# The last gate of a decoder layer as seven products of halves, with its weight sums made by DMA in DRAM

## The chip, the cores and the metric

The kernel runs on one core of one Trainium2 chip. The metric is the device time of one execution in microseconds (us). Lower is better. The engines are named as in the profile: PE (TensorE, with PEld for its weight loads), DVE (VectorE), ACT (ScalarE), POOL (GpSimd) and SP (SyncE, which here only issues DMAs). A DMA that SP issues goes into queue q1, one that POOL issues into queue q0; both are worked off by the same 16 DMA engines.

## The reference

One layer of a decoder: attention with forget gates, a normalisation, an MLP with a causal convolution over its gate, a second normalisation, and at the end a gated embedding that is added to the stream. 512 tokens, width 1024, MLP width 2816, all in float32.

```python
x = layer_norm(DEEPNORM_ALPHA * x + mix, ln_mix_g[i], ln_mix_b[i])
ffn = conv_ffn(x, ffn_w_up[i], ffn_conv_w[i], ffn_conv_b[i], ffn_w_down[i])
x = layer_norm(DEEPNORM_ALPHA * x + ffn, ln_ffn_g[i], ln_ffn_b[i])
gate = jax.nn.sigmoid(x @ ple_w_gate[i] + ple_b_gate[i])
x = x + gate * (p[i] @ ple_w_proj[i])
```

The change concerns `x @ ple_w_gate[i]`, a product of 512x1024 by 1024x1024, and the bias behind it.

## The kernel before, in words

**Products of float32.** Every operand is cut into a high part (rounded to fp32r by ACT) and a low part (the rest, subtracted by DVE). `three` (L147) issues three PE products for each block of 128 rows: high x high, high x low and low x high.

**Weights.** The class `Weights` holds a list of units of up to 128x1024 floats (512 KB). SP loads a unit into one of four `raw` buffers (L93), ACT cuts `whi` (L123) and DVE `wlo` (L129) into one of five pairs of buffers. A few units in the MLP have their low part made by an accumulating DMA that POOL issues (L126). SP's queue is in order, and so is each engine.

**The start.** SP loads the transposed input in eight blocks (`xraw<-xT`) between the first weights (`raw<-wv`, `raw<-wqk`), and ACT and DVE cut each block (L339, L340). PE computes the first values (`pv`), the first projections (`pp`), then the other values in two further rounds. In between, `keep_load` and `keep_sums` (L399 to L426) load pairs of blocks of the MLP's first weights (`ka`, `kb`), let DVE make sums of them (L421 to L424) and write these to DRAM (`kept`) for later. The sums stand in DVE's order between the cuts of weights and the release of the projections' PSUM banks (L460, L462). POOL makes two masks at the very start (L325, L326, L304) and then multiplies the attention's probabilities by their row sums' inverses (L499).

**The MLP** runs in four parts. For some blocks its products are already done as seven products of halves instead of eight (a scheme of the Strassen and Winograd kind: sums of quarters of both operands are multiplied, and the results combined). DVE and ACT follow an order written out in the code from its second block on (`manual_schedule`, L883); POOL and SP follow the scheduler.

**The end.** The last sums of the MLP (`r`), the second normalisation, the transposes of its result (`flip`, L644: PE transposes, ACT makes `x2h`, DVE `x2l`), seven of the eight halves of the embedding (`pl`, L988), and the gate (L998): for each of 2 column halves and 4 tiles of 128 tokens, 8 blocks of rows, three products each into one PSUM bank. DVE adds the bias (L1008), ACT takes the sigmoid (L1009), DVE multiplies by the embedding (L1014) and adds the stream (L1015), and SP stores. The last tile's second half runs in two quarters, with its embedding at the very end.

Of the kernel before, what the change touches and what calls it, by code (L numbers as in the profile page):

```python
# [9 lines left out]
F32 = mybir.dt.float32  # L10
F32R = mybir.dt.float32r
BF16 = mybir.dt.bfloat16
AF = mybir.ActivationFunctionType
# [3 lines left out]
P = 128  # L17
# [125 lines left out]
def trunk_layer(ctx: ExitStack, tc: tile.TileContext, xT, x2d, pT, wqk, wv0, wv1, wv2, bf, wo, wup, cwb,  # L143
# [108 lines left out]

    dram = ctx.enter_context(tc.tile_pool(name="dram", bufs=1, space=bass.MemoryType.DRAM))
    kept = {(j, q): dram.tile([P, 4, 512], F32, name=f"kept{j}_{q}") for j in KEPT for q in range(2)}
    u_up, u_dn = {}, [[] for _ in PAIRS]
    for part in range(4):
        fs = range(6 * part, min(6 * part + 6, NF))
# [32 lines left out]
    tl = slice(tiles[-1] * P, tiles[-1] * P + P)  # L290
    u_p1 = W.add(pT.rearrange("(k p) t -> p k t", p=P)[:, :, tl], n=2 * P, inner=P)
    u_pl1 = W.add(half_rows(wpl, 0, 2, 1), inner=512)


    zeros = base.tile([P, P], F32, name="zeros")
# [8 lines left out]
    nc.gpsimd.affine_select(ident, ones, pattern=[[1, P]], base=0, channel_multiplier=-1,  # L304
                            compare_op=ALU.is_equal, fill=0.0)

    neghalf = base.tile([P, 96], F32, name="neghalf")[:, :1]
    nc.vector.memset(neghalf, -0.5)


# [303 lines left out]
    def row(t, src):  # L614
        nc.sync.dma_start(t, src[0:1, :].to_broadcast([P, D]))
        return t
# [250 lines left out]

    before = None
    pending = []
    ordered = ExitStack()  # L870
    for part in range(4):
        ops = []
        slots = iter(CHUNKS[part] or ())

        def between():
            for _ in range(next(slots, 0)):
                next(before)

        for f in range(6 * part, min(6 * part + 6, NF)):
            q, j = f % 2, f // 2  # L880
            if f == 2:

                ordered.enter_context(tc.manual_schedule(  # L883
                    engines={mybir.EngineType.DVE, mybir.EngineType.Activation}))
            if q == 0 and j not in APART:
                E = hpool.tile([P, 8 * HALF], F32, tag="E", name=f"E{j}")
            if f == 0:
                a, b = slice(0, HALF), slice(HALF, S)
                up(0, 0, a)
                up(0, 1, a)  # L890
                up(1, 0, a, (3, x1h, x1l, xt))
                up(0, 0, b)
                up(0, 1, b)
                up(1, 0, b)
# [60 lines left out]
    x2l = post.tile([P, KD, S], F32R, tag="xl", name="x2l")  # L955
    for t in cut_tiles("X", 16, 1, "more", pool=hpool):
        extra.append(t.rearrange("p (a b) c -> p a (b c)", b=UNIT // HALF))
    for i, t in enumerate(tiles):
# [12 lines left out]
        if i == 0:  # L971
            W.cut_to(u_pl[1] + 1)
        if i > 1:
            flip(tiles[i - 2], x2h, x2l)


    pl = base.tile([P, NT, D], F32, tag="xl", name="pl")

    def embed(ps, up, ul, p0, pw, lo_c=0, w=512):

# [7 lines left out]
    for i, (n, t) in enumerate([(n, t) for n in range(2) for t in tiles][:-1]):  # L988
        ps = bank(f"pl{t}_{n}")
        embed(ps, u_p, u_pl[n], t * P, S)  # L990
        nc.scalar.activation(pl[:, t, n * 512:(n + 1) * 512], ps, AF.Copy)
        if i == 3:
            flip(0, x2h, x2l)


    bgs = row(cut_tiles("S", 4, 4, "bgs", F32)[0].rearrange("p a b -> p (a b)"), bg)

    def gate(n, t, lo_c=0, w=512):  # L998
        ps = bank(f"gt{n}{t}")[:, :w]
        c0 = slice(n * 512 + lo_c, n * 512 + lo_c + w)  # L1000
        tk = slice(t * P, (t + 1) * P)
        for k in range(KD):
            hi, lo = W.get(u_g[n][k // 2])
            c = slice(k % 2 * 512 + lo_c, k % 2 * 512 + lo_c + w)
            three(ps, hi[:, c], lo[:, c], x2h[:, k, tk], x2l[:, k, tk], k == 0, k == KD - 1,
                  weights_move=True)
        e = hpool.tile([P, S], F32, tag="a", name=f"ge{n}{t}_{lo_c}", bufs=2)[:, :w]
        nc.vector.tensor_add(e, ps, bgs[:, c0])  # L1008
        nc.scalar.activation(e, e, AF.Sigmoid)  # L1009
        return e  # L1010
# [7 lines left out]
    for n in range(2):  # L1018
        for t in tiles[:NT - n]:
            e = gate(n, t)  # L1020
            if n == 0 and t == tiles[0]:
                flip(1, x2h, x2l)
            finish(n, t, e, pl[:, t, n * 512:(n + 1) * 512])
    tz = tiles[-1]
    es = [gate(1, tz, c, 256) for c in (0, 256)]
    for e, c in zip(es, (0, 256)):
        ps = bank(f"pl{tz}_1{c}")[:, :256]
        embed(ps, u_p1, u_pl1, 0, P, c, 256)
        finish(1, tz, e, ps, c, 256)


def _layout(a):
# [45 lines left out]
```

## Time and profile before

| | |
|---|---|
| median of 3 runs | 651.94 us (651.73 to 652.17) |
| the profiled execution's own time | 651.7 us |
| its span | 650.0 us |
| PE busy | 644.2 us, 99% of the span |
| DVE busy | 520.8 us, 80% |
| ACT busy | 366.9 us, 56% |
| POOL busy | 93.6 us, 14% |
| moved by SP's queue | 105.77 MB |
| moved by POOL's queue | 3.15 MB |

Lines such as L152 are lines of the kernel. In a group, "out<-in xcount | busy, mean ns | idle before, releaser" gives the instructions of one line that write and read the named tiles, their busy time and their mean duration, then how long the engine sat idle before them and what ended that. In the chain of work that ended last, each row gives the start, the length and what ran. In the table of windows a row gives, for a stretch of time, the busy time and the number of instructions of PE, PEld, DVE, ACT and POOL, then the granted clock of PE, the mean busy share of the DMA engines and the GB/s moved. Starts of successive instructions of one engine can overlap with the end of the one before.

### The profile page before, as it was taken

How to read it: one execution, taken by the hardware profiler on the slowest of the kernel's cores; microseconds unless marked ns; L12 is line 12 of the kernel's file. 1: busy time of each engine (PE TensorE's matmuls, PEld its weight loads, DVE VectorE, ACT ScalarE, POOL GpSimd, SP SyncE). 2: the span in 40 equal slices, each digit the busy share in tenths (PEclk: the TensorE clock that was granted, in tenths of full speed). 3: DMA queues.
4: the chain of work that ended last, by engine and by line, in shares of the span. 5: the costliest groups of instructions: out<-in, count | busy, mean ns of one | idle time of the engine just before them, and what ended most of it. 6: DMA issues, size and time to landing. Idle time of an engine off the chain costs nothing.

```text
span 650.0 us, 10004 instructions
## 1 busy us (share of the span) xinstructions
PE 644.2 (99%) x3666; PEld 568.2 (87%) x3666; DVE 520.8 (80%) x854; ACT 366.9 (56%) x643; POOL 93.6 (14%) x85
## 2 busy tenths in 40 slices
PE   8999999999999999999999999999999999999997
PEld 7899888888888889889999988999988998888886
DVE  7764778988887599757899887789788998599464
ACT  6643777877785326946757554646545554425231
POOL 0000554454456021100000000000000000011000
PEclk9999999999999999999999999999999999999999
DMA  8764525445598315675665545663645562551321
GB/s 292 241 233 131 205 81 179 174 177 167 161 287 318 125 50 160 140 197 178 192 195 172 179 135 205 175 199 112 228 139 153 161 228 92 190 188 42 130 81 50
DMA packets 45858, 109.56 MB, mean 169 GB/s; under 512 B 4400, under 2 KB 8240, under 8 KB 45808
## 3 DMA queue, kind: packets, MB, share of 16 engines
q1 hardware_dynamic: 44944, 105.77, 49.7%
q0 software_dynamic: 864, 3.15, 2.6%
q8 instruction: 29, 0.48, 0.3%
q14 instruction: 21, 0.17, 0.1%
HBM read 96.19 MB, written 10.49 MB: 164 GB/s over the span
## 4 chain that ended last, share of the span: by engine, by line
PE 96%; DMA 2%; DVE 1%; SPq 1%; ACT 1%; issue 0%
PE g L152 18%; PE u L152 18%; PE pp L152 14%; PE x L152 8%; PE gt L152 7%; PE pv L152 7%; PE z L152 4%; PE r L152 3%; PE ap L152 3%; PE o L525 3%; PE t L512 2%; PE ao L152 2%; PE y L152 2%; PE s L475 2%; PE pl L152 2%; PE s L477 1%
## 5 line engine op out<-in xcount | busy, mean ns | idle before, releaser
L123 ACT ACTIVATE whi<-raw 128x1024 fp32r<-128x1024 f32 (+4 forms) x135 | 125.6, 938 | 87.0 <-PE pv L152 13.8
L129 DVE TENSOR_TENSOR wlo<-raw,whi 128x1024 fp32r<-128x1024 f32 (+4 forms) x130 | 137.5, 1067 | 31.4 <-ACT whi L123 30.4
L499 POOL TENSOR_SCALAR pr<-pr,rl 128x128 f32<-128x128 f32 (+1 forms) x64 | 75.5, 1195 | 132.1 <-DVE rl L495 132.1
L638 POOL TENSOR_TENSOR mv<-mv,neghalf 128x1 f32<-128x1 f32 x8 | 11.6, 1446 | 345.8 <-DVE mv L637 323.5
L152 PE MATMUL g<-x1h,whi 128*128 128x256 f32 (+1 forms) x168 | 54.7, 326 | 0.0
L152 PE MATMUL g<-x1l,whi 128*128 128x256 f32 (+1 forms) x168 | 54.4, 324 | 0.0
L152 PE MATMUL g<-x1h,wlo 128*128 128x256 f32 (+1 forms) x168 | 54.4, 324 | 0.0
L152 PE MATMUL u<-x1l,whi 128*128 128x256 f32 (+1 forms) x160 | 53.0, 331 | 0.0
L152 PE MATMUL u<-x1h,wlo 128*128 128x256 f32 (+1 forms) x160 | 53.0, 331 | 0.0
L152 PE MATMUL u<-x1h,whi 128*128 128x256 f32 (+1 forms) x160 | 53.0, 331 | 0.0
L152 PE MATMUL pp<-xh,wlo 128*128 128x512 f32 x128 | 50.5, 394 | 0.0
L152 PE MATMUL pp<-xh,whi 128*128 128x512 f32 x128 | 50.0, 391 | 0.0
L152 PE MATMUL pp<-xl,whi 128*128 128x512 f32 x128 | 50.0, 391 | 0.0
L491 ACT ACTIVATE pr<-s,nm 128x128 f32<-128x128 f32 (+1 forms) x64 | 33.5, 527 | 9.1 <-DVE nm L487 8.9
L152 PEld LDWEIGHTS g<-x1h,whi 128*128 128x128 f32 x168 | 32.0, 190 | 3.4 <-issue 0.7
L152 PEld LDWEIGHTS g<-x1l,whi 128*128 128x128 f32 x168 | 32.0, 190 | 2.6
L152 PEld LDWEIGHTS g<-x1h,wlo 128*128 128x128 f32 x168 | 32.0, 190 | 2.5
L152 PEld LDWEIGHTS u<-x1h,whi 128*128 128x128 f32 x160 | 30.4, 190 | 3.0
L152 PEld LDWEIGHTS u<-x1l,whi 128*128 128x128 f32 x160 | 30.4, 190 | 2.9
L152 PEld LDWEIGHTS u<-x1h,wlo 128*128 128x128 f32 x160 | 30.4, 190 | 2.8
L487 DVE CUSTOM_DVE_ANT_0 s<-s,mask 128x128 f32<-128x128 f32 (+1 forms) x64 | 30.0, 510 | 1.7 <-PE s L477 1.5
L123 ACT ACTIVATE whi<-side 128x512 fp32r<-128x512 f32 (+1 forms) x33 | 25.5, 782 | 9.7 <-PE u L152 3.6
(550 smaller groups left out, 1818.6 us busy)
## 6 DMA issues: line engine op xcount, KB each, us to landing
raw<-wup SPq DMA_DIRECT2D x34, 512.0 KB, 4.2
raw<-wdn SPq DMA_DIRECT2D x23, 512.0 KB, 3.8
raw<-wqk SPq DMA_DIRECT2D x16, 512.0 KB, 3.3
ka<-wup SPq DMA_DIRECT2D x8, 512.0 KB, 3.8
kb<-wup SPq DMA_DIRECT2D x8, 512.0 KB
kept<-kb SPq DMA_DIRECT2D x8, 512.0 KB, 3.5
kept<-ka SPq DMA_DIRECT2D x8, 512.0 KB, 3.1
raw<-wo SPq DMA_DIRECT2D x8, 512.0 KB, 4.3
```

Source lines behind the costliest of these rows:

```text
L123: self.nc.scalar.activation(hi[:, c:e], piece, AF.Copy)
L129: self.nc.vector.tensor_sub(lo[:, c:e], piece, hi[:, c:e].bitcast(F32))
L152: nc.tensor.matmul(ps, lhsT, rhs, start=start and n == 0, stop=stop and n == 2, skip_group_check=on)
L475: nc.tensor.matmul(ps[:, :n], QA[:, q], KA[:, :n], start=True, stop=False)
L477: nc.tensor.matmul(ps[:, :n], qb[0:68, q], kb[0:68, :n], start=False, stop=True)
L487: last_mask[:] = [nc.vector.tensor_tensor_reduce(ps[:, :w], ps[:, :w], mask[:, S - w:], -1.0, BIG, op0=ALU.add, op1=ALU.min, accum_out=nm[ ...
L491: nc.scalar.activation(pr[:, off:off + w], ps[:, :w], AF.Exp, bias=nm[:, i:i + 1], scale=-1.0, accum_out=ls[:, i:i + 1])
L499: nc.gpsimd.tensor_scalar_mul(pr[:, off:off + w], pr[:, off:off + w], rl[:, i:i + 1])
L512: nc.tensor.transpose(ps[:, w:w + P], pr[:, o:o + P], ident)
L525: nc.tensor.matmul(ps[:, q0:], V[:, j, h], p[:, o:o + w], start=j == 0 and n == 0, stop=j == NT - 1 and n == 1)
L638: nc.gpsimd.tensor_tensor(mv[:, 3:4], mv[:, 2:3], neghalf, op=ALU.pow)
```

## The change

The gate's product is split in halves three ways: rows of the weights (11, 12 above 21, 22), columns, and tokens (tiles 2 and 3 are the first half, 0 and 1 the second). Seven products of quarters replace eight, over 2 tiles each. In the code's names: x starts as the bias and takes a11 b11, then s2 t2, s3 t3 and a22 t4 on top; z starts as the sum of the two halves of the bias and takes s1 t1, then s4 b22; p2 is a12 b21. The bias is copied into PSUM by ACT before the first product, and products are added onto it. Copies of the sums in between are kept in SBUF (`g11`, `g12`, `g22`), and DVE combines them.

The sums of weights, t1 to t4, are made in DRAM tiles (`gt1` to `gt4`) by 16 DMAs that POOL issues: 8 plain copies and 8 accumulating ones, 512 KB each, in `gate_sums`. Ahead of each stands a copy of one column on ACT and one on POOL. The function is advanced twice for each of the MLP's blocks 6 to 13. The sums of the operand, s1 to s4, are made by DVE out of float32 copies of the transposed tiles, and cut by ACT and DVE (`second`).

```diff
+    gq = {f"t{n}": dram.tile([P, 4, 512], F32, name=f"gt{n}") for n in range(1, 5)}
+    steps = itertools.count(16)
+    def gate_sums():
...
+        for to, src in (("t1", "b11"), ("t2", "b22"), ("t1", "+b12"), ("t4", "b21"), ("t2", "+t1"),
+                        ("t3", "b22"), ("t4", "+t2"), ("t3", "+b12")):
+            for h in range(2):
+                m = next(steps)
+                nc.scalar.activation(small[:, m:m + 1], zeros[:, :1], AF.Copy)
+                nc.gpsimd.tensor_copy(small[:, m + 32:m + 33], small[:, m:m + 1])
+                if src[0] == "+":
+                    nc.gpsimd.dma_start(quad(to, h), quad(src[1:], h), accum_op=ALU.add)
+                else:
+                    nc.gpsimd.dma_start(quad(to, h), quad(src, h))
+                yield
...
-    u_g = [[W.add(half_rows(wg, 2 * j, 2, n), inner=512) for j in range(4)] for n in range(2)]
+    for g in ("b11", "b21", "t1", "t2", "b22", "t3", "t4"):
+        src = gq[g] if g in gq else half_rows(wg, 4 * int(g[1]) - 4, 4, int(g[2]) - 1)
+        u_g[g] = [W.add(src[:, 2 * j:2 * j + 2, :]) for j in range(2)]
...
+            if 6 <= f < 14:
+                next(beside)
+                next(beside)
...
+    def embedding(n, t, seed=None):
+        ps = bank(f"pl{t}_{n}", "six")
         embed(ps, u_p, u_pl[n], t * P, S)
         nc.scalar.activation(pl[:, t, n * 512:(n + 1) * 512], ps, AF.Copy)
+        if seed is not None:
+            nc.scalar.activation(ps, seed, AF.Copy)
+        return ps
...
+        s1, s2 = s12[:, :512], s12[:, 512:]
+        nc.vector.tensor_sub(s1, a21, pb)
+        nc.vector.tensor_sub(s2, s1, a11)
+        nc.scalar.activation(highs[0], s12, AF.Copy)
+        nc.vector.tensor_add(s4, a12, s2)
+        nc.vector.tensor_sub(s3, a11, a21)
+        nc.vector.tensor_sub(lows[0], s12, highs[0].bitcast(F32))
+        nc.vector.tensor_sub(x2l[:, 4:, tk], pb3, x2h[:, 4:, tk].bitcast(F32))
+        for v, c in ((s4, slice(0, 512)), (s3, slice(512, 1024))):
+            nc.scalar.activation(highs[1][:, c], v, AF.Copy)
+            nc.vector.tensor_sub(lows[1][:, c], v, highs[1][:, c].bitcast(F32))
...
     def finish(n, t, e, emb, lo_c=0, w=512):
         c0 = slice(n * 512 + lo_c, n * 512 + lo_c + w)
-        nc.vector.tensor_mul(e, e, emb)
-        nc.vector.tensor_add(y[:, t, c0], y[:, t, c0], e)
+        nc.scalar.activation(e[0], e[1], AF.Sigmoid)
+        nc.vector.tensor_mul(e[0], e[0], emb)
+        nc.vector.tensor_add(y[:, t, c0], y[:, t, c0], e[0])
...
+    x = [embedding(1, t, bgs[:, 0:512]) for t in firsts]
+    z = [embedding(1, t, b12) for t in seconds]
...
+    for i in range(2):
+        gate(x[i], i, "a11", "b11")
+        nc.scalar.activation(g11[i], x[i], AF.Copy)
+    second(1)
+    for i in range(2):
+        p2 = bank(f"p2{i}", "six")
+        gate(p2, i, "a12", "b21", on=False)
+        nc.vector.tensor_add(g11[i], p2, g11[i])
+        finish(0, firsts[i], (g11[i], g11[i]), emb(0, firsts[i]))
+    for i in range(2):
+        gate(z[i], i, "s1", "t1")
+        nc.scalar.activation(g22[i], z[i], AF.Copy)
...
```

POOL's order at the start of the program, before. The rows give the line, the operation, the tile written and the tile read, its size, and the semaphores waited for; `pr` are the probabilities of the first head, `rl` the inverses of their sums:

```order
L325 MEMSET mask 128x384
L326 ISA
L326 AFFINE_SELECT mask<-zeros 128x128 [waits DVE_49]
L304 AFFINE_SELECT ident<-ones 128x128 [waits DVE_49]
L499 TENSOR_SCALAR pr_704<-pr_704,rl_727 128x128 [waits DVE_49]
```

The same place on POOL now. `gt_71` is t1, `gt_72` t2, `gt_74` t4 and `gt_73` t3; a row with x2 stands for both halves; DMASW are the semaphores of POOL's own DMAs:

```order
L332 AFFINE_SELECT ident<-ones 128x128 [waits DVE_49]
L276 DMA gt_71<-wg 128x2x512 x2
L276 DMA gt_72<-wg 128x2x512 x2
L274 DMA gt_71<-wg 128x2x512 [waits DMASW0_49]
L274 DMA gt_71<-wg 128x2x512 [waits DMASW1_49]
L276 DMA gt_74<-wg 128x2x512 x2
L274 DMA gt_72<-gt_71 128x1024 [waits DMASW4_49,DMASW2_49]
L274 DMA gt_72<-gt_71 128x1024 [waits DMASW5_49,DMASW3_49]
L276 DMA gt_73<-wg 128x2x512 x2
L274 DMA gt_74<-gt_72 128x1024 [waits DMASW6_49,DMASW0_49]
L274 DMA gt_74<-gt_72 128x1024 [waits DMASW7_49,DMASW1_49]
```

All 16 DMAs (two more accumulates into `gt_73` follow) stand between the masks and the first multiplication; they wait for each other alone. POOL's 16 one-column copies stand elsewhere, behind the accumulating loads of the MLP:

```order
L126 DMA wlo_2974<-wup 128x1024 [waits DVE_49,Activation_49]
L126 DMA wlo_3017<-wup 128x1024 [waits DMASW0_49,PE_49,Activation_49]
L638 TENSOR_TENSOR mv<-mv,neghalf 128x1 [waits DVE_49,Pool_49] x4
L1074 UNCONDITIONAL_BRANCH
L1074 ISA [waits barrier_Pool_Activation_PE_DVE_SP_gather]
```

```order
L126 DMA wlo_2978<-wup 128x1024 [waits DVE_49,Activation_49]
L126 DMA wlo_3021<-wup 128x1024 [waits DMASW0_49,DMASW5_49,PE_49,Activation_49]
L272 COPY neghalf<-neghalf 128x1 [waits Activation_49] x16
L667 TENSOR_TENSOR mv<-mv,neghalf 128x1 [waits DVE_49,Pool_49] x4
L1191 UNCONDITIONAL_BRANCH
```

The first of these two is before, the second now: the copies came in there, and the DMAs did not move with them.

DVE's order where the gate begins, before: `wlo` are the low parts of the gate's weights, `ge` the gate of the first tile.

```order
L129 TENSOR_TENSOR wlo149_6149<-raw149_5925,whi149_6148 128x1024 [waits DMAHW6_49]
L129 TENSOR_TENSOR wlo150_6161<-raw150_5927,whi150_6160 128x1024 [waits DMAHW7_49]
L129 TENSOR_TENSOR wlo151_6173<-raw151_6119,whi151_6172 128x1024 [waits DMAHW0_49]
L129 TENSOR_TENSOR wlo152_6185<-raw152_6152,whi152_6184 128x1024 [waits DMAHW1_49,Activation_49]
L1008 TENSOR_TENSOR ge02_0_6196<-gt02_6147,bgsh_6144 128x512 [waits DMAHW2_49,PE_49]
```

The same place now: `bgsl` holds s1 and s2 of the third tile, `s430` its s4 and s3, `sg0` their low parts, `nt` the transposed tile in PSUM.

```order
L129 TENSOR_TENSOR wlo149_6139<-raw149_5982,whi149_6138 128x1024 [waits DMAHW6_49]
L1064 TENSOR_TENSOR bgsl_5934<-w21h_6136,nt_6169 128x512 [waits Activation_49]
L1068 TENSOR_TENSOR s430l_6183<-x2th_5931,w21h_6136 128x512
L1065 TENSOR_TENSOR bgsl_5934<-bgsl_5934,x2th_5931 128x512 [waits DVE_49]
L1070 TENSOR_TENSOR x2l_5928<-nt_6169,x2h_5927 128x4x128
L1067 TENSOR_TENSOR s430h_6182<-x2th_5931,bgsl_5934 128x512 [waits DVE_49]
L1073 TENSOR_TENSOR sg0l_6181<-s430l_6183,morel_5930 128x512 [waits Activation_49]
L1069 TENSOR_TENSOR sg0h_6180<-bgsl_5934,moreh_5929 128x1024 [waits Activation_49]
L1073 TENSOR_TENSOR sg0l_6181<-s430h_6182,morel_5930 128x512 [waits Activation_49]
L129 TENSOR_TENSOR wlo150_6238<-raw150_5984,whi150_6237 128x1024 [waits DMAHW7_49]
L129 TENSOR_TENSOR wlo151_6242<-raw151_6080,whi151_6241 128x1024 [waits DMAHW0_49]
L129 TENSOR_TENSOR wlo152_6256<-raw152_6143,whi152_6255 128x1024 [waits DMAHW1_49]
```

The eight operations on the operand's sums came in between the cuts of units 149 and 150. Up to the end of the MLP the orders of PE, DVE and SP are the same as before, and ACT's has the one-column copies added.

More of the change, by code (lines that the diff above doesn't have):

```diff
@@ L305, in trunk_layer @@
                             compare_op=ALU.is_equal, fill=0.0)
-    neghalf = base.tile([P, 96], F32, name="neghalf")[:, :1]
+    small = base.tile([P, 96], F32, name="neghalf")
+    neghalf = small[:, :1]
     nc.vector.memset(neghalf, -0.5)
@@ L869, in trunk_layer @@
     pending = []
+    beside = gate_sums()
     ordered = ExitStack()
@@ L957, in trunk_layer @@
         extra.append(t.rearrange("p (a b) c -> p a (b c)", b=UNIT // HALF))
+    firsts, seconds = tiles[:2], tiles[2:]
+    x2t = {t: v.rearrange("p a (b c) -> p (a b) c", c=P)
+           for t, v in zip(firsts, cut_tiles("S", 4, 4, "x2t", F32))}
+    bgs, s12 = [v.rearrange("p a b -> p (a b)") for v in cut_tiles("S", 4, 4, "bgs", F32)]
+    row(bgs, bg)
     for i, t in enumerate(tiles):
@@ L973, in trunk_layer @@
         if i > 1:
-            flip(tiles[i - 2], x2h, x2l)
+            flip(tiles[i - 2], x2h, x2l, x2t)
+        if i == 2:
+            W.cut_to(u_g["b11"][0] + 1)
     pl = base.tile([P, NT, D], F32, tag="xl", name="pl")
+    b12 = pl[:, tz, 0:512]
+    nc.vector.tensor_add(b12, bgs[:, 0:512], bgs[:, 512:1024])
     def embed(ps, up, ul, p0, pw, lo_c=0, w=512):
@@ new lines, in embedding, with second @@
+        return ps
+    whole = cut_tiles("A", 2, 3, "w21", F32)
+    sg = []
+    def second(i):
+        t = seconds[i]
+        tk = slice(t * P, (t + 1) * P)
+        pa, pb = [bank("nt", "two") for _ in range(2)]
+        for n, ps in enumerate((pa, pb)):
+            for k in range(4):
+                nc.tensor.transpose(ps[:, k * P:(k + 1) * P], y[:, t, (4 * n + k) * P:(4 * n + k + 1) * P], ident)
+        a21 = whole[i].rearrange("p a b -> p (a b)")
+        nc.scalar.activation(a21, pa, AF.Copy)
+        pb3 = pb.rearrange("p (k c) -> p k c", c=P)
+        nc.scalar.activation(x2h[:, 4:, tk], pb3, AF.Copy)
+        a11, a12 = [x2t[firsts[i]][:, 4 * n:4 * n + 4, :].rearrange("p k c -> p (k c)") for n in range(2)]
+        lows = [v.rearrange("p a b -> p (a b)") for v in cut_tiles("S", 4, 4, f"sg{i}")]
+        highs = [v[:, (3, 0)[i], :] for v in extra]
+        s4, s3 = [v.rearrange("p a b -> p (a b)") for v in cut_tiles("A", 2, 3, f"s43{i}", F32)]
+        s1, s2 = s12[:, :512], s12[:, 512:]
[9 more added lines that the diff above has]
+            nc.vector.tensor_sub(lows[1][:, c], v, highs[1][:, c].bitcast(F32))
+        sg.append({g: [v[m // 2][:, m % 2 * 512:m % 2 * 512 + 512].rearrange("p (k c) -> p k c", c=P)
+                       for v in (highs, lows)] for m, g in enumerate(("s1", "s2", "s4", "s3"))})
@@ new lines, in gate @@
+    def gate(ps, i, a, u, on=True, lo_c=0, w=512):
+        if a in ("a11", "a12", "a22"):
+            t = (firsts, seconds)[int(a[1]) - 1][i]
+            n = 4 * int(a[2]) - 4
+            xs = [v[:, n:n + 4, t * P:(t + 1) * P] for v in (x2h, x2l)]
+        else:
+            xs = sg[i][a]
+        for k in range(4):
+            hi, lo = W.get(u_g[u][k // 2], 3)
+            c = slice(k % 2 * 512 + lo_c, k % 2 * 512 + lo_c + w)
+            three(ps[:, lo_c:lo_c + w], hi[:, c], lo[:, c], xs[0][:, k, :], xs[1][:, k, :], k == 0 and not on,
+                  k == 3, weights_move=True, on=on)
@@ L1024, in trunk_layer, with emb, a_tile @@
[L1024 to L1027, printed above, removed]
+    def emb(n, t):
+        return pl[:, t, n * 512:(n + 1) * 512]
+    def a_tile(name):
+        return hpool.tile([P, S], F32, tag="a", name=name, bufs=2)
+    W.cut_to(u_g["b11"][1] + 1)
+    for t in firsts:
+        embedding(0, t)
+    embedding(0, seconds[0])
+    second(0)
+    x = [embedding(1, t, bgs[:, 0:512]) for t in firsts]
+    z = [embedding(1, t, b12) for t in seconds]
@@ new lines, in trunk_layer @@
+    g12, g22 = [[v.rearrange("p a b -> p (a b)") for v in cut_tiles("A", 2, 3, n, F32)] for n in ("g12", "g22")]
+    g11 = [a_tile(f"g11_{i}") for i in range(2)]
+    for i in range(2):
[7 more added lines that the diff above has]
+        finish(0, firsts[i], (g11[i], g11[i]), emb(0, firsts[i]))
@@ new lines, in trunk_layer @@
+    for i in range(2):
+        gate(z[i], i, "s1", "t1")
+        nc.scalar.activation(g22[i], z[i], AF.Copy)
+    for i in range(2):
+        gate(x[i], i, "s2", "t2")
+        nc.scalar.activation(g12[i], x[i], AF.Copy)
+    for i in range(2):
+        gate(z[i], i, "s4", "b22")
+        nc.vector.tensor_sub(g12[i], z[i], g12[i])
+        finish(1, firsts[i], (g12[i], g12[i]), emb(1, firsts[i]))
+    for i in range(2):
+        gate(x[i], i, "s3", "t3")
+        nc.vector.tensor_sub(g22[i], g22[i], x[i])
+        finish(1, seconds[i], (g22[i], g22[i]), emb(1, seconds[i]))
@@ L1028, in trunk_layer @@
+    gate(x[0], 0, "a22", "t4")
+    finish(0, seconds[0], (a_tile("g21_0"), x[0]), emb(0, seconds[0]))
+    for c in (0, 256):
+        gate(x[1], 1, "a22", "t4", True, c, 256)
+    e = a_tile("g21_1")
+    for c in (0, 256):
+        ps = bank(f"pl{tz}_0{c}", "two")[:, :256]
         embed(ps, u_p1, u_pl1, 0, P, c, 256)
-        finish(1, tz, e, ps, c, 256)
+        finish(0, tz, (e[:, c:c + 256], x[1][:, c:c + 256]), ps, c, 256)
 def _layout(a):
```

31 lines of the change are left out of this document (7 added, 24 removed).

## The prediction

> **What bounds the kernel now.** I read the page first, then the chain that ended last, and only then the stages that the change touches: the last 60 us and, because of where the new transfers stand, the first 60.
>
> ```profile
> span 650.0 us, 10004 instructions
> PE 644.2 (99%) x3666; PEld 568.2 (87%) x3666; DVE 520.8 (80%) x854; ACT 366.9 (56%) x643; POOL 93.6 (14%) x85
> PE 96%; DMA 2%; DVE 1%; SPq 1%; ACT 1%; issue 0%
> ```
>
> TensorE (PE) is busy for 99% of the span and is 96% of the chain that ended last, so a matrix product taken away is time, unless its place is taken by a wait. The chain over the last stretch (start, length, what):
>
> ```profile
> 599.80 5.44 PE gt L152 x24
> ...
> 606.12 38.41 PE gt L152 x192
> 644.53 1.05 PE pl L152 x7
> ```
>
> 24 products of 128x512 take 5.44 us, 0.2268 us each, without a gap. The gate has 216 of them because the code runs its last tile in halves: 168 whole products and 48 half ones, as much as 192 whole.
>
> The start is bound otherwise. The first chain pieces and the stages by window (PE, PEld, DVE, ACT, POOL busy, clock, DMA share, GB/s):
>
> ```profile
> 4.07 4.56 DMA raw<-wv
> 9.37 6.82 PE pv L152 x52
> ...
> 30.14 4.88 PE pv L152 x28
> ```
>
> ```profile
> 0.00:5.00 5.00, 3.89 (x17) 2.74 (x18) 3.55 (x14) 2.54 (x4) 1.15 (x7) 1.00 0.55 154
> 5.00:10.00 5.00, 4.24 (x28) 3.43 (x28) 3.35 (x6) 3.22 (x6) 0.00 (x0) 1.00 0.98 304
> 10.00:16.00 6.00, 6.00 (x50) 6.00 (x49) 4.51 (x7) 4.61 (x7) 0.00 (x0) 1.00 1.02 393
> ```
>
> From 5 to 16 us the 16 DMA engines are full, with the loads of xT, wv and wqk alone. The chain goes through a load until 8.6 us, and after that PE is only just behind them.
>
> **The products taken away.** Before: 4 token tiles x 2 column halves x 8 blocks of rows x 3 parts = 192 whole products. After: 7 products of halves x 2 tiles x 4 blocks x 3 = 168. The embedding keeps 14 half-tile groups and the transposes stay 32. So 24 x 0.2268 = **5.4 us** less on PE, all of it in a stretch where PE never stops.
>
> **What the end has to hide.** VectorE (DVE) and ScalarE (ACT) get more work there. The groups of the last 61 us and DVE's windows:
>
> ```profile
> L129 DVE TENSOR_TENSOR wlo<-raw,whi 128x1024 fp32r<-128x1024 f32 (+1 forms) x10 | 11.0, 1140 | 1.4 <-ACT whi L123 1.4
> L1008 DVE TENSOR_TENSOR ge<-gt,bgsh 128x512 f32<-128x512 f32 (+1 forms) x9 | 5.7, 630 | 14.0 <-PE gt L152 13.9
> L655 DVE TENSOR_TENSOR x2l<-nt,x2h 128x512 fp32r<-128x512 f32 x6 | 4.0, 677 | 0.4 <-ACT x2h L654 0.4
> ```
>
> ```profile
> 590.00:600.00 10.00, 10.00 (x50) 8.38 (x49) 10.00 (x15) 5.05 (x10) 1.45 (x1) 1.00 0.19 52
> 600.00:610.00 10.00, 10.00 (x50) 8.38 (x49) 5.72 (x8) 4.12 (x6) 0.00 (x0) 1.00 0.57 170
> 610.00:620.00 10.00, 10.00 (x45) 8.28 (x45) 4.48 (x8) 2.62 (x4) 0.00 (x0) 1.00 0.14 54
> 620.00:630.00 10.00, 10.00 (x46) 8.26 (x44) 6.96 (x9) 3.40 (x5) 0.00 (x0) 1.00 0.29 105
> 630.00:640.00 10.00, 10.00 (x51) 8.52 (x50) 3.48 (x6) 1.09 (x2) 0.00 (x0) 1.00 0.14 52
> ```
>
> DVE gains 6 weight cuts (14 units for 8) at 1.14, 8 operand sums, 4 cuts of 512 and one bias sum at about 0.63, and 2 cuts of 1024 at 1.14; it loses 2 x2l cuts and 2 of 8 bias additions. That is 6.8 + 8.2 + 2.3 - 2.6 = 14.7 us more on 30.6 busy of 50. 45.3 us in the 44.6 that remain is tight, though some of it (the first cut, the bias sum) can lie before 590. Followed row by row, the order puts the operand sums of the first tile before the cuts of units 150 to 152, whose products start only after two whole gates; by these durations each cut is ready 0.5 to 3 us ahead. I take 0.3 us of waits, bounds 0 to 2.5 (a quarter of the sums and cuts, 8 us, coming late). ACT has 16 us of work in these 50 and gets some 20 more (copies, seeds of the bias, cuts): covered. If the cover goes, each late cut costs PE its lateness. POOL does nothing there. The final multiply, add and store are the same; the sigmoid that now reads PSUM is done before the last embedding.
>
> The 16 one-column copies on ACT, in the MLP, and on POOL behind them cost nothing: ACT is 56% busy and nobody waits for them.
>
> **Where the 16 transfers really stand.** The copies were meant to pace them, but no data ties a transfer to its copy. In the built order the copies stand behind the MLP's accumulates, and all 16 transfers stand right behind the two masks, with no wait on any compute engine. In the profile of before POOL has this there:
>
> ```profile
> 1.51 0.28 POOL L304 TENSOR_SCALAR_AFFINE_SELECT ident<-ones 128x128 f32<-128x128 f32 x1
> 68.54 4.80 POOL L499 TENSOR_SCALAR pr<-pr,rl 128x128 f32<-128x128 f32 x4 [66.75 <-DVE rl L495]
> ```
>
> So the transfers start at about 1.8 us, into the full engines. The trace has no DRAM to DRAM transfer; the nearest are six accumulating loads in the MLP, and one stretch shows them against SP's queue (packets, MB, share of 16 engines):
>
> ```profile
> q0 software_dynamic: 432, 1.55, 70.7%
> q1 hardware_dynamic: 450, 1.17, 29.1%
> ...
> wlo<-wup POOLq DMA_DIRECT2D x1, 512.0 KB, 9.0
> ```
>
> That is 277 to 288 us, engines full. Packet for packet the two queues take turns (432 against 450), and the accumulating queue holds the engines for 71% of the time: 0.707 x 11 / 1.55 = 5.0 us of all 16 engines per MB, against 2.7 for plain loads beside it. The queue SP fills at the start does this from 5 to 16 us, and these are what it carries until the last xT (issues up to 11.5 us):
>
> ```profile
> q1 hardware_dynamic: 2294, 3.87, 99.9%
> ```
>
> ```profile
> xraw<-xT SPq DMA_DIRECT2D x7, 256.0 KB, 3.7
> raw<-wqk SPq DMA_DIRECT2D x2, 512.0 KB
> raw<-wv SPq DMA_DIRECT2D x3, 272.0 KB, 5.0
> raw<-wv SPq DMA_DIRECT2D x2, 136.0 KB
> xraw<-xT SPq DMA_DIRECT2D x1, 192.0 KB
> xraw<-xT SPq DMA_DIRECT2D x1, 64.0 KB
> ```
>
> 3.87 MB in 11 us is 2.8 us per MB. 4160 KB are 4.26 MB, of which 0.77 (154 GB/s for 5 us) have landed by 5 us, so 3.5 MB, about 2,070 packets, are still to come. If POOL's queue gets a packet for each of these, it moves its first four copies (1,088 packets, 2.1 MB), the two accumulates into t1 (544, 1.05 MB) and most of the next two copies: 2.1 x 2.8 + 1.05 x 5.0 + 0.85 x 2.8 = 13.5 us. That is the upper bound for the delay of the last xT. The lower is zero, if POOL's queue always had gaps where SP's is empty. Between them: over 250 to 285 us, with waits between its transfers, POOL's queue held
>
> ```profile
> q0 software_dynamic: 764, 2.80, 44.1%
> ```
>
> and at 44% the 10 us of loads would take 10 / 0.56, 8 us more. I take 10: four copies can be issued without waiting for anything, so there are fewer gaps than there.
>
> The Trainium skill (DMA: Bandwidth & Descriptors, Anatomy of one DMA, SWDGE path) prices a software DMA at 2.0 us plus its bytes at 436 GB/s, with nothing extra for accumulating: an estimate of 3.2 us for 512 KB, where the row has 9.0 to landing. By that page the interleaved megabytes would cost at most 9.2 us, and the forecast would be some 3 us lower; the rows are of this chip and kernel, and I go by them.
>
> What the delay does: the last xT is cut and used at once.
>
> ```profile
> 16.18 0.61 ACT L339 ACTIVATE xh<-xraw 128x512 fp32r<-128x512 f32 x1
> 17.45 0.69 DVE L340 TENSOR_TENSOR xl<-xraw,xh 128x512 fp32r<-128x512 f32 x1
> 17.72 0.67 PE L152 MATMUL pv<-whi,xh 128*128 128x272 f32 x4
> ```
>
> The cut is ready at 16.8, PE takes it at 17.72: about 1 us of slack. PE's order is fixed, and what stands behind the last xT takes until 30.14 whatever came before. So **9 us** of the 10 shift everything (0 to 12.5).
>
> After that, the value products and their loads run beside the rest of POOL's transfers, 33 us of engine time in all (4.2 MB x 2.8 + 4.2 MB x 5.0). The cover is long but has one weak place: DVE's in-order sums of ka and kb.
>
> ```profile
> 26.37 0.67 DVE L421 TENSOR_TENSOR ka<-kb,ka 128x512 f32<-128x512 f32 x1
> 37.36 0.69 DVE L460 SCALAR_TENSOR_TENSOR QB<-pp,QA 64x512 fp32r<-64x512 f32 x1
> ```
>
> ```profile
> 46.64 0.33 PE L152 MATMUL pv<-whi,xh 128*128 128x384 f32 x1
> ```
>
> Behind L421 stand the projection's release at 37.4 and the cuts for the second half of the values, which PE starts at 46.64: 8.6 us of cover, and 9 more by the shift. Between the last xT and kb stand four loads of wv and ka: with kb about 1,370 packets (256 for a wv load in rows of 1.5 KB, 128 for one of ka or kb in rows of 4). At a packet for a packet POOL's queue puts in the rest of its copies and the next five accumulates, 1.25 MB x 2.8 + 2.7 MB x 5.0 = 17 us at most, so kb is 10 to 27 us late. Up to 17.6 is covered, and the middle, 18.5, is not quite. I take **1.5 us** of waiting, bounds 0 to 9.
>
> POOL itself is blocked by four dependent steps of about 9 us, to some 40 us; its first multiply is needed at 68.5. Covered, unless DRAM accumulates take twice as long.
>
> **Sum**, against the profiled execution's own 651.7 us (span 650.0): 651.7 - 5.4 + 0.3 + 9 + 1.5 = **657.1 us**. The median of the three runs is 651.94, 0.2 above that run; a difference under about 0.2%, 1.3 us, is not told from none.
>
> **Rivals.**
> 1. *The start hides the transfers.* POOL's queue lets SP's packets through, or its descriptors come slowly, so that the last xT is at most 1 to 4 us late. For: how the queues take turns was seen in one stretch alone, with larger rows on SP's side and with SP's queue perhaps not always full. Against: engines at 0.98 to 1.02 from 5 to 16 us, and 432 against 450 packets. It gives 651.7 - 5.4 + 0.3 + 0 to 4 = 646.6 to 650.6, and turns from gain to loss at a delay of about 5 us. The case that the transfers run in the MLP after all, as the copies intend, gives the same 646.6; against it stands the built order. Chance 0.21.
> 2. *DVE blocked behind kb.* kb is over 24 us late, DVE stands at its sum, and PE runs dry before the second values: 9 + 8 instead of 9 + 1.5, 663.6 (662 to 666). For: in-order sums, loads behind POOL's larger packets. Against: POOL's accumulates wait for each other, which leaves SP's queue alone in between. Chance 0.12.
> 3. *A draw*: the delay just about eats the gain, 650.6 to 653.2. Chance 0.07.
>
> The forecast itself, 653.2 to 662, has 0.60. That gives slower 0.72, same 0.07, faster 0.21. The range runs from the hidden case's lower end, 646.3, to 665, which takes in the blocked DVE; the likeliest case alone is 653.2 to 662.
>
> **What would show it.** Right: q0 packets from about 5 us on and over by 60; PE with several us of idle time before 30 us, released by DMA through whi or xh; the second values begun at 55 to 58 us instead of 46.6; the gate stretch 5 us shorter with PE full. Rival 1: at 46 to 51 us. Rival 2: PE waiting for DVE between 45 and 60 us, DVE waiting for kb. Wrong in the end stage: PE waits over 1 us for wlo or for the operand sums after 590 us. Wrong altogether: transfers seen in the MLP, or a PE that finishes the gate no earlier than its start moved.

## The result and the profile after

The changed kernel takes 669.43 us (median of 4 runs, 668.5 to 671.79), the kernel before in the same comparison 652.06 (651.73 to 652.17). The ratio is 1.027 (95% interval 1.024 to 1.030): slower by 17.4 us. The forecast had the direction, but 669.4 lies above its range of 646.3 to 665.0.

The profiled execution (own time 670.07 us), its span, its engines and the shares of its chain:

```profile
span 668.3 us, 10057 instructions
PE 644.9 (96%) x3630; PEld 567.0 (85%) x3630; DVE 533.1 (80%) x870; ACT 384.1 (57%) x685; POOL 117.4 (18%) x117
PE 79%; DMA 13%; ACT 3%; DVE 3%; issue 1%; SPq 1%; ACTq 0%; DVEq 0%
```

PE was idle for 650.0 - 644.2 = 5.8 us before and is for 668.3 - 644.9 = 23.4 now: 17.6 more. It is busy for 0.7 us more, although 5.4 us of products are gone, so the products that are left took 6.1 us longer. 17.6 - 5.4 + 6.1 = 18.3, the difference of the spans.

Where the time came from is told by one landmark: the products of the MLP's last sums (`r`), which stand in the same place of PE's order in both. This is their row (durations, then first and last start), before and after:

```profile
L152 PE MATMUL r<-whi,s9h x16: 388/390/477, 565.3 to 586.3; 128*128 128x512 f32 x16
```

```profile
L152 PE MATMUL r<-whi,s9h x16: 388/389/476, 588.6 to 609.6; 128*128 128x512 f32 x16
```

The last of them starts 23.3 us later. From there to the end it is 63.7 us before and 58.7 now: the new gate gains 5.0 us. So everything is lost ahead of that point, and the windows of the first 100 us hold it:

```profile
5.00:10.00 5.00, 1.39 (x11) 1.17 (x10) 0.97 (x2) 0.91 (x2) 0.32 (x1) 0.84 0.97 290
10.00:16.00 6.00, 3.45 (x13) 3.13 (x14) 2.18 (x4) 2.07 (x4) 1.59 (x2) 0.50 1.04 382
16.00:22.00 6.00, 6.00 (x39) 6.00 (x39) 2.94 (x6) 3.45 (x5) 0.00 (x0) 0.78 1.08 325
...
70.00:80.00 10.00, 3.88 (x18) 2.93 (x17) 3.99 (x4) 3.55 (x4) 1.15 (x1) 0.83 0.97 237
80.00:100.00 20.00, 14.62 (x56) 11.96 (x57) 13.32 (x31) 11.92 (x27) 6.24 (x6) 0.74 0.57 211
```

There are two holes in PE's work, one from 5 to 16 us and one from 70 to 90; in and behind each the granted clock is down to 0.5 to 0.84. From 100 us on PE is full again. The chain of waits through both holes:

```profile
3.12 9.11 DMA xraw<-xT
...
13.64 9.30 DMA xraw<-xT
...
43.10 13.70 DMA kept<-kb
56.82 7.78 DMA raw<-wv
...
65.09 8.85 DMA raw<-wqk
...
76.36 6.07 DMA raw<-wqk
...
84.85 0.48 DVE V L411
85.33 0.04 issue
85.38 8.07 PE pp L152 x24
```

The first hole is the late input that was forecast: the cut of the last block of the input starts 9.1 us late (16.18 before).

```profile
25.25 0.62 ACT L368 ACTIVATE xh<-xraw 128x512 fp32r<-128x512 f32 x1
```

The scores of the first head, which stand right behind the last values, begin at 71.5 us where they began at 63.3:

```profile
L504 PE MATMUL s<-KA,QA x8: 278/311/767, 71.5 to 93.9; 128*128 128x256 f32 x4, 128*128 128x384 f32 x2, 128*128 128x512 f32 x2
```

That is 8.2 us. The second hole makes the other 15, and it was not forecast. This is the start of the same projection in the chain of before:

```profile
64.74 5.46 PE pp L152 x24
```

It now starts 20.6 us late, 12.4 more than the scores, and its 24 products, at the low clock behind the hole, take 2.6 us longer. Its weights (`raw<-wqk`) are loaded from 65.09 on. The last step of the chain is DVE: `V`, for which PE waits, stands in DVE's order behind the cuts of these late weights. SP's own waits up to 95 us (in total, how often, the longest) name what held the load of values before them:

```profile
SPq L93 <- DMA kept<-kb: 10.8, 1, 10.8
```

SP's queue from 26 us on, before and after (start, length, line, transfer), shows it in place:

```profile
29.00 0.34 SPq L404 DMA_DIRECT2D kept<-kb  x1
31.59 0.33 SPq L404 DMA_DIRECT2D kept<-ka  x1
31.98 0.43 SPq L93 DMA_DIRECT2D raw<-wv  x1
...
40.37 9.26 SPq L93 DMA_DIRECT2D raw<-wqk  x4
```

```profile
43.10 0.34 SPq L433 DMA_DIRECT2D kept<-kb  x1
45.70 0.33 SPq L433 DMA_DIRECT2D kept<-ka  x1
56.82 0.38 SPq L93 DMA_DIRECT2D raw<-wv  x1
...
65.09 3.08 SPq L93 DMA_DIRECT2D raw<-wqk  x3
```

`kb` lies in one of the four raw buffers. The next load of values goes into that buffer, so it waits until the store `kept<-kb` has read it. Before, the store is issued at 29.00 and the load follows at 31.98. Now the store takes 13.7 us among POOL's transfers, the load waits, and behind it in SP's order the loads of wqk wait too: they go from 40.37 to 65.09, 24.7 us, while PE was 8.2 us late. Some 14 of these 24.7 us are the late `kb` itself, whose store is issued at 43.10 instead of 29.00, and nearly 11 are SP's wait for the slow store. From 40 to 57 us POOL's queue holds the engines for 79.0% of the time and SP's for 24.7%. The queues up to 90 us (packets, MB, share of 16 engines):

```profile
q1 hardware_dynamic: 6952, 14.51, 46.3%
q0 software_dynamic: 2816, 8.39, 46.1%
```

The 16 transfers held all engines for 0.461 x 90 = 41.5 us, not the 33 of the prediction, and they were not over by 60 us. POOL issues the last one here:

```profile
72.28 1.15 POOL L274 DMA_DIRECT2D gt<-wg  x1 [9.94 <-issue]
```

### The profile page after: what moved, and what is told of

Read it like the earlier page. It is cut to its first block, busy times and chain, and to the rows that moved or that the text cites. A ratio compares the mean times of both kernels' runs of the same rounds, so it can differ in the third digit from the quotient of the medians.

```text
span 668.3 us, 10057 instructions
## 1 busy us (share of the span) xinstructions
PE 644.9 (96%) x3630; PEld 567.0 (85%) x3630; DVE 533.1 (80%) x870; ACT 384.1 (57%) x685; POOL 117.4 (18%) x117
## 4 chain that ended last, share of the span: by engine, by line
PE 79%; DMA 13%; ACT 3%; DVE 3%; issue 1%; SPq 1%; ACTq 0%; DVEq 0%
PE g L152 17%; PE u L152 17%; PE pp L152 12%; PE x L152 7%; PE z L152 4%; PE r L152 3%; PE ap L152 3%; DMA xraw<-xT 3%; PE o L554 3%; PE t L541 2%; PE ao L152 2%; DMA raw<-wqk 2%; DMA kept<-kb 2%; PE y L152 2%; DMA kb<-wup 2%; PE pl L152 2%
## 5 line engine op out<-in xcount | busy, mean ns | idle before, releaser
L123 ACT ACTIVATE whi<-raw 128x1024 fp32r<-128x1024 f32 (+4 forms) x141 | 132.2, 943 | 115.8 <-DMA raw<-wv 26.5
L129 DVE TENSOR_TENSOR wlo<-raw,whi 128x1024 fp32r<-128x1024 f32 (+4 forms) x136 | 144.5, 1073 | 52.8 <-ACT whi L123 52.4
L667 POOL TENSOR_TENSOR mv<-mv,neghalf 128x1 f32<-128x1 f32 x8 | 11.6, 1447 | 211.6 <-DVE mv L666 189.3
L152 PE MATMUL pv<-whi,xh 128*128 128x384 f32 (+1 forms) x96 | 31.5, 340 | 6.5 <-ACT whi L123 6.2
L152 PEld LDWEIGHTS pp<-xh,wlo 128*128 128x128 f32 x128 | 24.6, 192 | 12.7 <-DVE V L411 7.5
## 6 DMA issues: line engine op xcount, KB each, us to landing
kept<-ka SPq DMA_DIRECT2D x8, 512.0 KB, 14.2
```

What stands on the lines that cost most here:

```text
L123: self.nc.scalar.activation(hi[:, c:e], piece, AF.Copy)
L129: self.nc.vector.tensor_sub(lo[:, c:e], piece, hi[:, c:e].bitcast(F32))
L152: nc.tensor.matmul(ps, lhsT, rhs, start=start and n == 0, stop=stop and n == 2, skip_group_check=on)
L667: nc.gpsimd.tensor_tensor(mv[:, 3:4], mv[:, 2:3], neghalf, op=ALU.pow)
```

## The experiments

Two theories stood at first. By theory 1 the sum of the engines' time decides: 41.5 us of transfers do not fit into the idle time of the first stretch. By theory 2 the order decides: a few loads that come late or wait for a slow store. Each ratio is to the kernel before on the same chip (651.97 to 652.13 us).

**The transfers held back (held).** Each transfer is ordered on POOL behind its copy, and so runs where the copy runs.

```diff
-                nc.gpsimd.tensor_copy(small[:, m + 32:m + 33], small[:, m:m + 1])
-                if src[0] == "+":
+                step = nc.gpsimd.tensor_copy(small[:, m + 32:m + 33], small[:, m:m + 1])
+                with tc.issue_after(step.ins):
+                    if src[0] == "+":
```

> The 16 transfers truly wait for their one-column copies, so they run in the MLP. Theory 1, the sum of the transfer time: the 16 transfers hold all 16 DMA engines for 41.5 us (46.1% of the first 90 us of the changed kernel), and what does not fit into the idle time of the engines pushes the loads back; in 300 to 450 us the engines of before are at 0.51 to 0.62, so some 65 us of 150 are idle and 41.5 fit: 646 to 648 us, and the start is again that of before (second values at 46.6 us). Theory 2, the order of the loads (late first loads, then one load that waits for a slow store of the sums kept): it has nothing to act on here either, 646 to 648. Rival 3, transfers of this kind slow the loads wherever they stand: over 650, with PE waits in the MLP.

Measured: 650.78 us (649.9 to 651.93), ratio 0.998 (0.997 to 0.999). The first scores begin at 64.0 us (63.3 before), and the loss is gone: it came from where the transfers stood. But it misses the 646 to 648 and has what rival 3 named, over 650 and PE waits in the MLP. PE's waits in this kernel:

```profile
PE u L152 <- DVE E L822: 1.1, 1, 1.1
...
PE pl L152 <- DVE g22h L1137: 1.0, 1, 1.0
PE g L152 <- DVE a L751: 0.4, 1, 0.4
```

Two transfers per block crowd the MLP: from 360 to 440 us the DMA engines are at 0.88 where they were at 0.58 before, and PE waits for 1.5 us for DVE. In the end PE waits 1.0 us, because `s3 t3` has to be read by DVE before `a22 t4` is added onto it. (The trace names PSUM banks after their last tenant, `pl`.)

**No transfers (none).**

```diff
-                nc.gpsimd.tensor_copy(small[:, m + 32:m + 33], small[:, m:m + 1])
-                if src[0] == "+":
-                    nc.gpsimd.dma_start(quad(to, h), quad(src[1:], h), accum_op=ALU.add)
-                else:
-                    nc.gpsimd.dma_start(quad(to, h), quad(src, h))
+                pass
...
-    for g in ("b11", "b21", "t1", "t2", "b22", "t3", "t4"):
-        src = gq[g] if g in gq else half_rows(wg, 4 * int(g[1]) - 4, 4, int(g[2]) - 1)
-        u_g[g] = [W.add(src[:, 2 * j:2 * j + 2, :]) for j in range(2)]
+    for to in ("b11", "b21", "t1", "t2", "b22", "t3", "t4"):
+        g = {"t1": "b11", "t2": "b22", "t3": "b12", "t4": "b21"}.get(to, to)
+        src = half_rows(wg, 4 * int(g[1]) - 4, 4, int(g[2]) - 1)
+        u_g[to] = [W.add(src[:, 2 * j:2 * j + 2, :]) for j in range(2)]
```

> The 16 transfers are left out and the gate reads plain quarters of its weights in place of their sums; the rest is as in the changed kernel. All theories: the end alone, 651.9 - 5.4 + 0.3 = 646 to 648. The difference between held and this kernel is what the transfers cost in the MLP: under 0.7 by theories 1 and 2, over 3 by rival 3.

Measured: 648.90 us (648.23 to 650.54), ratio 0.995 (0.994 to 0.997). That is above the 646 to 648: the end alone gains 3.2 us, not 5.1; its profile has 1.6 us of PE waiting for that read of `s3 t3`, inside the 0 to 2.5 us that the prediction gave the end. Held is 1.9 above it, between the 0.7 of theories 1 and 2 and the 3 of rival 3, so twice a block the transfers do cost something in the MLP; the last runs below show that this comes from the crowding.

**The transfers after the first loads (late).** The transfers stand behind a POOL copy that reads the last cut of the input; the rest is as in the changed kernel.

```diff
     value_rows(0)
+    x_in.append(nc.gpsimd.tensor_copy(small[:, 90:91], xl[:, KD - 1, S - 1:].bitcast(F32)).ins)
...
+                with tc.issue_after(x_in[0]):
```

> The first transfer waits for the cut of the last block of the input, so that the first loads (to some 17 us) have the engines to themselves. Theory 1: before had 16.0 us of idle engine time from 16 to 60 us and 7.4 more to 70, against 41.5 us of transfers, so the loads are pushed back by 18 to 25 us all the same, only later: 664 to 671 us, and the first values end as in before. Theory 2: the 8.2 us lost by the first loads are saved and the 13.5 us behind the slow store stay: 659 to 663. My prediction's main term, the late first loads alone: 646 to 650.

Measured: 668.07 us (667.47 to 669.35), ratio 1.025 (1.023 to 1.026). The number is theory 1's, but the rows are not. The first hole is gone as all said (14.21 us of PE work by 16 us, 14.12 before). What stops PE later are two things in order, not one in bytes: its waits, and SP's for the store:

```profile
PE t L544 <- POOL pr L531: 8.8, 4, 6.6
PE pp L152 <- DVE V L413: 7.6, 1, 7.6
```

```profile
SPq L93 <- DMA kept<-kb: 10.1, 2, 6.7
```

Started some 17 us later, POOL's chain of dependent transfers lasts beyond 90 us, and the first multiplications of the probabilities stand behind it on POOL. This run doesn't tell the theories apart.

**kb in a buffer of its own (kbuf).** Three padded tiles are made smaller to find the space.

```diff
-                  base.tile([P, UNIT], F32, name=f"kb{j}_{q}", tag="raw", bufs=RAW_BUFS))
+                  ap.tile([P, UNIT], F32, name=f"kb{j}_{q}", tag="keepb", bufs=1))
```

> The changed kernel, with the second block of each kept sum in a buffer of its own instead of one of the four raw buffers, so that no load of values waits for its store (10.8 us of SP's time in the changed kernel). Theory 1: the engines are full all the same, so the time stays within 3 us of the changed kernel, 666 to 671. Theory 2: the wait goes and with it most of the second stall of 13.5 us: 656 to 661.

Measured: 663.05 us (659.58 to 666.39), ratio 1.017 (1.012 to 1.021), below the one theory and above the other; the profile is of the slowest of its four runs. The edit did not do what was meant: the wait is not gone but has moved to the next load of `kb`, which now waits for the same store and has the loads of wqk behind it.

```profile
SPq L439 <- DMA kept<-kb: 13.0, 1, 13.0
```

**The transfers alone (bstart).** Before, with the call of `gate_sums` put behind the masks, without its copies.

```diff
                             compare_op=ALU.is_ge, fill=NEG)
+    for _ in gate_sums():
+        pass
```

> The kernel before, gate and all, with nothing added but the 16 transfers behind the two masks; nothing reads what they write. If the loss of the changed kernel is all in the transfers' place (theory 1, and theory 2 too), this shows it whole: the changed kernel's start is 23.3 us late (last sums of the MLP begun at 609.6 us against 586.3), so 652.1 + 23 = 673 to 677. Rival: a part of the loss is in the new gate, or the new gate hides some of it: under 672.

Measured: 673.55 us (670.68 to 677.28), ratio 1.033 (1.030 to 1.037). 21.6 us of loss without the new gate, where the changed kernel loses 17.4 with it: the loss is the transfers' alone, and the gate takes back some 4.

**Half of the transfers (half).**

```diff
+                if h:
+                    yield
+                    continue
```

> The changed kernel with the eight transfers of the first halves alone (the other halves of the sums are left out, plain quarters are read there). Theory 1: 20.7 us of engine time go into the 25.7 us that the engines of before are idle up to 70 us, so the wait for the second projections' weights goes; what stays is the delay of the first loads, 6 to 8 us, which PE can't make up: 648.9 + 6 to 8 = 654 to 657. Rival, a loss in proportion to the transfers: half of 20, 659 to 661.

Measured: 659.97 us (658.18 to 661.4), ratio 1.013 (1.011 to 1.015). The second hole is gone, as theory 1 said; the number is the rival's, because the first one is larger than in the changed kernel. The chain goes from the values to the scores without a stop, 11.6 us late (63.44 before):

```profile
41.75 33.30 PE pv L152 x192
75.06 0.23 PE s L508 x2
```

So the rival's number is luck. SP's queue shows why the second hole is gone:

```profile
43.98 0.34 SPq L437 DMA_DIRECT2D kept<-kb  x1
...
46.96 0.43 SPq L93 DMA_DIRECT2D raw<-wv  x1
```

The store is issued as late as in the changed kernel (43.10), but POOL's queue moves nothing from 40 us on, and the load of values follows 3.0 us behind the store, as it did before, with no wait for it. So a late `kb` alone makes no hole; it takes the slow store.

**Plain copies (plain).** `accum_op=ALU.add` is taken out of the accumulating transfers.

> The changed kernel with the eight accumulating transfers made plain copies (so the sums of weights are left out), same order, bytes and waits. In the changed kernel POOL's queue moved 212 GB/s at a share of 0.81 with copies alone (5 to 10 us), 3.8 us of all engines per MB, and 172 at 1.01 with accumulates (55 to 60 us), 5.9 per MB. By these the 16 copies cost 8.39 x 3.8 = 32 us against 41.5, and theory 1 gives 9 us less than the changed kernel: 657 to 662. Rival, an accumulate costs no more than a copy from DRAM to DRAM: 668 to 671.

Measured: 664.82 us (663.02 to 667.49), ratio 1.020 (1.018 to 1.022). Between the two again, but the price is plain. The queues up to 90 us:

```profile
q1 hardware_dynamic: 7197, 15.45, 49.3%
q0 software_dynamic: 2304, 8.39, 27.6%
```

Sixteen copies hold the engines for 24.8 us, 2.96 us per MB. The eight accumulates of the changed kernel then cost 41.5 - 12.4 = 29.1 us for 4.19 MB, 6.9 us per MB. The second hole isn't there: POOL's queue is empty by 50 us, the store is issued at 51.52, and the load behind it follows at 54.51. But the first has grown: the chain has the scores at 81.57, 18.1 us late.

```profile
54.88 26.69 PE pv L152 x154
81.57 0.23 PE s L504 x2
```

The traces suggest why cheaper transfers delay the first loads more. A transfer that ends sooner lets POOL issue the next one sooner: all 16 are issued by 38.41 us here, 10 in the changed kernel. From 20 to 40 us POOL's queue holds the engines for 63.8% of the time here, 53.1% in half and 42.6% in the changed kernel, and the first delays have the same order (18.1, 11.6, 8.2 us). No run tried it by itself.

**The store out of the way (kfree, bkfree).** kbuf, and besides the second round of loads of the sums kept and the first round of stores move from the second values to the first head's scores and after. The same two edits on the kernel before are the measure.

```diff
-    keep_sums()
-    keep_load()
     value_rows(2)
...
-            if s == 0 and h != 2:
+            if s == 0 and h != 2 or h == 3:
                 keep_sums()
                 keep_load()
```

> The changed kernel with the kept sums taken out of the way: kb in a buffer of its own, and the second round of loads and the first round of stores moved from the second values to the scores of the first head and after, so no load of values or of projections stands behind a store or waits for its buffer. In the changed kernel the scores begin 8.2 us late and the next projection 15 us later still. Theory 1 (what the engines carry decides): 2.1 MB at some 2.7 us per MB, 5.7 us, are gone from the stretch, so 9 of the 15 us stay: 662 to 666. Theory 2 (the order decides: the slow store and what waits for it): the 15 us go but for 2, 655 to 659.

> The kernel before with the same two edits on the kept sums, as the measure for the run above: no store delays it and PE has no wait there to lose, so 651 to 653 by both theories. If this moves by more than 1 us, the run above is read against it.

Measured: kfree 654.66 us (653.11 to 657.63), ratio 1.004 (1.003 to 1.006); bkfree 651.99 (651.31 to 652.26), ratio 0.999 (0.998 to 1.000). The edits change nothing by themselves, and take 14.8 of the 17.4 us out of the changed kernel. The DMA engines are as full as in the changed kernel (in steps of 10 us 0.89 to 1.08 from 30 to 70, 0.96 to 1.04 there), POOL's queue carries the same 8.39 MB at 44.9%, yet the second hole is nearly gone; PE's chain passes from the values to the next projection in under 3 us:

```profile
40.47 33.15 PE pv L152 x191
73.62 1.06 ACT whi L123
74.71 1.23 DVE wlo L129
75.93 0.48 DVE V L411
76.45 5.74 PE pp L152 x24
```

```profile
L152 PE MATMUL r<-whi,s9h x16: 388/389/476, 576.6 to 597.6; 128*128 128x512 f32 x16
```

The landmark is 11.3 us late instead of 23.3. With the quick stores of half and plain, that settles the second hole for theory 2: it is the loads behind the slow store of kept sums. Theory 1's 662 to 666, which allowed for the 2.1 MB moved out of this stretch, is out.

**One transfer to a block (spread, spreadonly).** The version that the runs pointed to: held, with the transfers one to each of blocks 6 to 21.

```diff
-            if 6 <= f < 14:
-                next(beside)
-                next(beside)
+            if f >= 6:
+                next(beside)
```

spread besides puts the products `s3 t3` ahead of `s4 b22`.

> A version meant to keep the gain: the transfers held behind their copies, one for each of the MLP's blocks 6 to 21 instead of two for each of 6 to 13, and in the gate s3 t3 goes before s4 b22, so that DVE has 5.4 us instead of 2.7 to read x before a22 t4 is added onto it. Held twice a block they cost 1.5 us of PE waits in the MLP, and the wait for that read was 0.3 to 1.6 us: with both gone, 648.9 - 1.4 = 647 to 649. If the transfers cost as much spread out: 649 to 650.5.

> The transfers held one to a block as in the run called spread, with the gate's order as in the changed kernel. If the 3.6 us between held and spread come from the spreading of the transfers, the MLP has no PE wait here and the end has its 0.3 to 1.6: 648 to 649. If they come from the gate's order: 649.5 to 651.

Measured: spread 647.18 us (647.02 to 648.74), ratio 0.993 (0.992 to 0.995); spreadonly 647.45 (646.46 to 648.9), ratio 0.992 (0.991 to 0.994). Both beat both kernels, before by 4.7 to 4.8 us; spread is inside its 647 to 649, spreadonly is even below its 648 to 649. Spreading does it: neither trace has a PE wait from 200 us to the end, with 16 more transfers in it, and the MLP's windows of spread are full:

```profile
250.00:400.00 150.00, 150.00 (x963) 136.90 (x963) 125.20 (x180) 93.83 (x148) 15.21 (x19) 1.00 0.67 194
400.00:550.00 150.00, 150.00 (x898) 134.09 (x897) 130.63 (x185) 81.79 (x135) 12.87 (x19) 1.00 0.71 201
```

The gate's order changes nothing that these runs can tell.

## Why the prediction was wrong

- **The products taken away and the end: right.** Forecast -5.4 + 0.3; the changed kernel's end is 5.0 us shorter, and the waits of the end were 0.3 us there (up to 1.6 in other runs, within the bounds of 0 to 2.5).
- **Where the transfers stand: right.** They start at the program's start, and with them held in the MLP the loss is gone (held, spread, spreadonly); bstart shows it without the gate.
- **The first loads: right.** Forecast 9 us out of 10 for the last block of the input, bounds 0 to 12.5; measured 8.2 out of 9.1 in the changed kernel, 11.6 in half. The bound does not hold for every such kernel: with plain copies it was 18.1.
- **After that: the step that failed.** The prediction said that the cover is long but has one weak place, DVE's sums of ka and kb, and took 1.5 us for it, bounds 0 to 9. The values did lose nothing there: kb's first sum was 14.1 us late, which is inside the forecast 10 to 27 and under the 17.6 of cover, and the values ran without a stop. The real place was one step on, in SP's queue: the store of the same sums holds a raw buffer, and the loads of values and projections stand behind it. It cost 15 us, 12.4 of standing and 2.6 of slower products behind. The prediction listed the loads between the last xT and kb, and asked who waits for the sums on DVE; it did not follow the buffer of `kb` to its next user, nor the store that has to read it. That order was in the trace of before, where the store is issued at 29.00 and the load at 31.98; that the store would take 13.7 us instead of at most 3 was not.
- **The price of an accumulate: too low.** 5.0 us per MB from one stretch; the changed kernel shows 6.9. Copies were right (2.8 for 2.96). With it the end of the transfers was too early: the prediction had POOL blocked to some 40 us and its queue done by 60, and the last issue is at 72.28. That this let the late store fall among the transfers fits half and plain, where POOL's queue was done before it; the price was not changed alone.
- **Rival 2 was near, and wrong.** It put kb's lateness on DVE, with 663.6 us. kb's sum was late (its first step at 40.47 where it was 26.37), but PE did not wait for it. Where PE did wait for DVE, later, DVE stood before the cuts of the late wqk.
- **The clock was left out.** The prediction added idle time alone. The products behind the holes ran at a granted clock of 0.5 to 0.84 and took 6.1 us longer. Only 2.6 of these can be put to the kernel's time: at 23.6 us, when the clock was back at 1.00, PE had stood another 0.3 us for a block of the input, so at the first hole the loads decided and not the clock.

## What to carry to other kernels

Background transfers are placed by the built order, not by the loop in which they are written: tie them by data or order to the place meant, and spread them. Where they run beside loads, do not only add up bytes; walk the loading queue and ask of each buffer which store or sum still has to read it, because one slow store holds every load behind it. A lost microsecond near the start of a kernel that PE bounds is lost for good.

## What the runs showed of the hardware

- An accumulating transfer from DRAM to DRAM held the engines for 6.9 us per MB in the changed kernel, a copy for 2.96 (41.5 against 24.8 us for the same 8.39 MB). In half it was 6.0: a share of 20.8% of 90 us for 4.19 MB, less the copies at 2.96.
- The store `kept<-ka` of 512 KB on SP's queue landed 3.1 us after its issue with POOL's queue empty (before, half), and 14.2 to 17.2 us after it with accumulates in POOL's queue (changed kernel, bstart, kbuf).
- SP's issue of these two loads took 0.46 and 0.34 us before, and 2.30 us each while the engines were full with both queues:

```profile
27.05 2.30 SPq L439 DMA_DIRECT2D ka<-wup  x1
29.45 2.30 SPq L439 DMA_DIRECT2D kb<-wup  x1
```

- A stop of PE can cost more than its length: the granted clock was 0.50 from 10 to 16 us and 0.74 on average from 80 to 100, and the 24 products behind the second hole took 8.07 us instead of 5.46. The Trainium skill (TensorE: Matmul & The Clock Gate, Part 1: The HAM clock gate) says that the array is at half rate when it has been idle and comes back after a few us of work; the windows agree.
- Left open: the first delay varies from 8.2 us (changed kernel) over 11.6 (half) to 18.1 (plain) and follows neither the bytes nor the price of the transfers. It goes with the share of POOL's queue from 20 to 40 us, which suggests the cause but does not show it.
